# Two pool groups in steps beside the last two attention heads, squares through PSUM, key and query halves by transfer

## The chip, the cores and the metric

The kernel runs on one core of one Trainium2 chip. The metric is device microseconds of one execution. Before the change three runs took 2717.0 to 2720.67 us, median 2718.06 us.

The engines are named as in the profile: PE multiplies matrices (PEld is its weight load), DVE is the vector engine, ACT the activation engine, POOL the general engine, SP the engine that issues nearly all DMA transfers, in program order, as do all engines their own work.

## The reference, cut to what matters

One step of a network of two layers on 128 context tokens and 1024 latent tokens of width 1024, all in float32. Layer 0 is the mixer that the change touches:

```python
h = rmsnorm(x) * (1 + mod[1]) + mod[0]          # mod = silu(c) @ w_mod + b_mod, six parts of 1024
q, k, v, p = even_project(h, w_in, ...)         # 512 columns each; q and k get an rmsnorm per head (8 heads of 64)
a = neighbourhood_attention(q, k, v, cached keys and values, rpb)   # 8 rows x 16 columns, plus 256 cached keys
for g, w in enumerate((2, 4, 8, 16)):           # four pool groups of 128 channels
    d = window_mean(p[g], w) - p[g]
    y[g] = (d @ pool_w[g]) * pool_scale[g]
x = x + mod[2] * (concat(a, y) @ w_out)
x = x + mod[5] * conv_ffn(rmsnorm(x) * (1 + mod[4]) + mod[3])
```

Layer 1 has a convolution module in place of attention and pool, and the same feed-forward part.

## The kernel before, in words

Activations lie with features on the 128 partitions: eight tiles of 128 x 1154 (128 context tokens, 2 columns of gap, 1024 latent tokens). Each float32 product is three matmuls, of a high and a low part (`whi`, `wlo`, `hhi`, `hlo`): high x high, high x low, low x high. A weight unit of 128 x 1024 is loaded by SP, its high part is made by ACT, its low part by POOL (`wunit`, L246 to L258).

Layer 0 runs in `mixer0` in this order.

1. `start0` loads x, squares each of its eight tiles on ACT (L482) and sums the squares over features on PE (L484: nine matmuls with one column per tile, 72 in all). It also computes mod parts 0 and 1 in four quarters (`quarters`, L497 to L528; `modps` L502, `modt` L508), each of which gives two tiles of `hhi` and `hlo`.
2. `project_v` makes v in two passes over the eight tiles (L606 to L609). Beside it, and later, mod group (0, 1) is loaded and multiplied (`mod_group`, L292: sixteen loads of 512 KB, `mraw`, and 32 matmuls, `modps` L303).
3. The first query and key pair (`project_qk`), with the four pool groups in the order `PF = (1, 3, 2, 0)` between (`project_p`: 72 projection matmuls L454, window sums on DVE L554, high and low parts, then nine `pw` matmuls L584). Each pool group's last matmuls stand behind the next group's projection.
4. `attention`, 40 units: eight heads with one context unit and four latent units each. A unit has scores (`C`, `S`), a softmax, transposes (`tp` L852) and the weighted sum (`O`). In every unit `filler` is called twice. It advances the query and key projection of the next pair in heads 0 to 5, and mod group (0, 2) in heads 6 and 7 (`RM = 1` step per call). mod group (0, 2) uses six buffers, two each of the tags `wraw`, `whi` and `wlo`.
5. `split_half` prepares a head's operands: the keys in f32r once on the head's own 64 partitions (L678, ACT) and once on the other 64 (L680, DVE), the low part of the keys (POOL), the queries on the own partitions and their low part on the others (ACT, DVE), and a copy of the queries into `qm` (L691, POOL).
6. `trunk` reads back the eight tiles `cat` (four of attention, four of pool), splits them (L1286, L1287), and begins with the output projection: three output tiles together, the eight inputs in the order `[4, 5, 6, 7, 0, 1, 2, 3]`.

A scheduler with a model of times sets the final order on each engine. A transfer on SP that waits holds those behind it.

Of the kernel before, what the change touches and what calls it, by code (L numbers as in the profile page):

```python
# [39 lines left out]
PL = 8  # L40
PL0 = PL + NCTX + PL
PW = PL0 + NLAT + PL
WINS = (2, 4, 8, 16)
# [77 lines left out]
MS = 4  # L121
MT = 0
MI = 1.1
PF = (1, 3, 2, 0)
SEQ = (0, 0), (0, 1), (1, 0), (1, 1), (2, 0), (2, 1)
KP = 0
LP = 3
PP = 2
RM = 1
RQ = 3  # L130
EK = 0
ER = 1
# [26 lines left out]
class Beside:  # L159
# [24 lines left out]
    def finish(self):  # L184
        while self.parts:
            self.step()


class Kern:
# [43 lines left out]

    def wload(self, src):
        raw = self.wp.tile([P, 1024], F32, tag="wraw", name=self.nm("wraw"), bufs=2)
        self.nc.sync.dma_start(raw, src)
        for dst, lo in self.stores:
            self.nc.sync.dma_start(dst, lo)
        self.stores = []
        return raw  # L240

    def wunit(self, src, raw=None, eng=None, keep=None, kept=None):


        nc = self.nc
        if raw is None:  # L246
            raw = self.wload(src)
        hi = self.wp.tile([P, 1024], F32R, tag="whi", name=self.nm("whi"), bufs=self.wbufs)
        lo = self.wp.tile([P, 1024], F32R, tag="wlo", name=self.nm("wlo"), bufs=self.wbufs)
        if kept is not None:  # L250
# [206 lines left out]
    def start0(self, up, hp, ap, evac):  # L457


        nc = self.nc  # L460
        mm = nc.tensor.matmul
        xs, raws, wv = [], [], []
        nc.sync.dma_start(self.consts, self.i["consts"])
        for k in range(KT):
            x = up.tile([P, TS], F32, tag="u", name=f"x0_{k}")
# [5 lines left out]
        for i in range(16):  # L471
            raw = hp.tile([P, T], F32, tag="h", name=self.nm("mraw"))
# [2 lines left out]
            if i in (3, 7):  # L475
                wv.append(self.wload(self.i["wv"][i // 4]))
        st = [tok0(j) for j in range(9)]
        ms = self.psa.tile([P, 512], F32, tag="aux", name=self.nm("ms"))
        for k in range(KT):
            sq = ap.tile([P, 2, 640], F32, tag="prob", name=self.nm("sq"), bufs=2)  # L480
            sq = sq.rearrange("p a b -> p (a b)")[:, :T]
            nc.scalar.activation(sq, xs[k], AF.Square)  # L482
            for j, o in enumerate(st):
                mm(ms[:, j:j + 1], sq[:, o:o + P], self.cst("on"), start=k + j == 0, stop=k == KT - 1 and j == 8)  # L484
        r = self.rsqrt(ms[:, :9], 9)
        rb = self.psm.tile([P, 3, 512], F32, tag="mm3", name=self.nm("rb"))
        for j in range(9):
# [49 lines left out]
    def project_p(self, g, hhi, hlo, up):  # L537

        nc = self.nc
        w = WINS[g]  # L540
        ps = self.proj(self.wunit(self.i["wab"][g]), hhi, hlo)
        p = up.tile([P, TS], F32, tag="u", name=self.nm("p"))
        for o, n in ((0, PL), (PL + NCTX, PL), (PL0 + NLAT, PL)):
            nc.gpsimd.memset(p[:, o:o + n], 0.0)
        for pv, sv in self.psegs(ps, p, PL, PL0):
            nc.scalar.activation(sv, pv, AF.Copy)
        s, lo, hi = p, 0, PW
        step = 0
        while 2 ** (step + 1) <= w:
            a = 1 if step == 0 else 2 ** (step - 1)  # L550
            b = 0 if step == 0 else a
            nlo, nhi = lo + a, hi - b
            s2 = up.tile([P, TS], F32, tag="u", name=self.nm("ps"))
            nc.vector.tensor_tensor(s2[:, nlo:nhi], s[:, nlo - a:nhi - a], s[:, nlo + b:nhi + b], op=ALU.add)  # L554
            s, lo, hi = s2, nlo, nhi
            step += 1
        d = up.tile([P, TS], F32, tag="u", name=self.nm("pd"))
        nc.gpsimd.memset(d[:, NCTX:L0], 0.0)
        for (o, n, dst) in ((PL, NCTX, 0), (PL0, NLAT, L0)):
            nc.vector.scalar_tensor_tensor(d[:, dst:dst + n], s[:, o:o + n], 1.0 / w, p[:, o:o + n],  # L560
                                           op0=ALU.mult, op1=ALU.subtract)
        e0 = sum(x - 1 for x in WINS[:g])
        hw = w // 2
        edge = self.cst("edge")
        for (o, n, dst) in ((PL, NCTX, 0), (PL0, NLAT, L0)):
            for (c, m, eo) in ((0, hw, e0), (n - hw + 1, hw - 1, e0 + hw)):
                if m == 0:
                    continue
                tmp = self.cp.tile([P, 8], F32, tag="pedge", name=self.nm("pedge"), bufs=2)
                nc.vector.tensor_tensor(tmp[:, :m], s[:, o + c:o + c + m], edge[:, eo:eo + m], op=ALU.mult)  # L570
                nc.vector.tensor_tensor(d[:, dst + c:dst + c + m], tmp[:, :m], p[:, o + c:o + c + m],
                                        op=ALU.subtract)
        dh = up.tile([P, TS], F32R, tag="u", name=self.nm("pdh"))
# [4 lines left out]
        def finish():  # L578
            ps = self.psm.tile([P, 3, 512], F32, tag="mm3", name=self.nm("pw"))
            sl = slice(g * P, (g + 1) * P)  # L580
            for w_, x, a, b in ((self.pwhi, dh, True, False), (self.pwhi, dl, False, False),
                                (self.pwlo, dh, False, True)):
                for c, (o, n) in enumerate(CH):
                    nc.tensor.matmul(ps[:, c, :n], w_[:, sl], x[:, o:o + n], start=a, stop=b)  # L584
            y = up.tile([P, TS], F32, tag="u", name=self.nm("py"))
            for pv, sv in self.row3(ps, y):
                nc.scalar.activation(sv, pv, AF.Identity, scale=self.par("psc", g))
            nc.sync.dma_start(self.cat[4 + g], y[:, :T])
        return finish

    def project_v(self, hhi, hlo, ready, wv, sp, between):

# [71 lines left out]
    def split_half(self, q, k, b, new, res):  # L664


        nc = self.nc

        def lat(t):
            return t.rearrange("p (r g c) -> p r g c", g=4, c=16)  # L670

        def blk(t):
            return t.rearrange("p (g r c) -> p r g c", g=4, c=16)

        own = slice(64 * b, 64 * b + 64)
        oth = slice(64 - 64 * b, 128 - 64 * b)
        ks = new("ks")
        nc.scalar.activation(ks[own, :], k[own, :T], AF.Copy)  # L678
        yield
        nc.vector.tensor_copy(ks[oth, :], k[own, :T])  # L680
        nc.gpsimd.tensor_tensor(self.km[b][own, :], k[own, :T], ks[own, :].bitcast(F32), op=ALU.subtract)
        yield
        qs = new("qs")
        nc.scalar.activation(qs[own, :NCTX], q[own, :NCTX], AF.Copy)
        nc.scalar.activation(blk(qs[own, L0:T]), lat(q[own, L0:T]), AF.Copy)
        yield
        nc.vector.tensor_tensor(qs[oth, :NCTX], q[own, :NCTX], qs[own, :NCTX].bitcast(F32), op=ALU.subtract)
        nc.vector.tensor_tensor(blk(qs[oth, L0:T]), lat(q[own, L0:T]), blk(qs[own, L0:T]).bitcast(F32),
                                op=ALU.subtract)
        for o, e in ((0, NCTX), (L0, T)):  # L690
            nc.gpsimd.tensor_copy(self.qm[b][own, o:e], qs[own, o:e])  # L691
        res[b] = (qs, ks)
        yield

# [461 lines left out]
    def mixer0(self, dp):  # L1156
        tc, nc, I, cp = self.tc, self.nc, self.i, self.cp
        with ExitStack() as l0:
# [83 lines left out]
    def trunk(self):  # L1242
# [11 lines left out]
        with ExitStack() as st:  # L1254
# [242 lines left out]
```

## Time and profile before

| | us |
|---|---|
| median of three runs | 2718.06 |
| profiled execution, its time | 2718.41 |
| profiled execution, its span | 2716.6 |
| PE busy in the span | 2635.2 (97%) |
| DVE busy | 1605.9 (59%) |
| ACT busy | 1122.9 (41%) |
| POOL busy | 1260.9 (46%) |

The span runs from the first to the last instruction, and 1.8 us of the profiled execution lie around it. The mixer of layer 0 ends at 537.5 us, where the first matmul of the output projection begins. A "record" is one entry of PE in the trace; a float32 matmul of PE that isn't f32r has two. The granted clock (PEclk) is a share of 2.4 GHz, and 0.5 is the lower level of 1.2 GHz.

### The profile page before, as it was taken

The numbers are of one execution on the slowest core, as the hardware profiler recorded it, in microseconds if no ns is written. First come the engines' busy times: TensorE is split into PE (matmuls) and PEld (weight loads), VectorE is DVE, ScalarE is ACT, GpSimd is POOL, SyncE is SP. The second block draws the span as 40 slices with busy tenths as digits, with TensorE's granted clock in tenths as the row PEclk, the third lists the DMA queues.
The fourth block names the chain that finished last, engine by engine and source line by source line (L and its number), as shares of the span: only waits on it lengthen the run. The fifth ranks groups of instructions, "written<-read, shape, count | busy, mean of one in ns | idle before, by whom it ended". The sixth has DMA issues, their size and how long they took to land.

```text
span 2716.6 us, 38806 instructions
## 1 busy us (share of the span) xinstructions
PE 2635.2 (97%) x15108; PEld 2379.8 (88%) x15108; DVE 1605.9 (59%) x2456; ACT 1122.9 (41%) x1743; POOL 1260.9 (46%) x752
## 2 busy tenths in 40 slices
PE   8999998889999999999999999999999999999999
PEld 6688887688999999988998789989999999888887
DVE  2236777575476757663997854369974334444444
ACT  3325766525422222245555363555324323433332
POOL 1323444146433232225555353699756544655553
PEclk9999998999999999999999999999999999999999
DMA  7622214364446555544434553232222222433232
GB/s 266 198 76 69 56 53 131 92 223 146 145 150 202 175 174 192 193 147 156 142 133 144 178 179 116 85 88 77 70 74 70 77 85 71 125 93 93 93 95 92
DMA packets 137815, 341.17 MB, mean 126 GB/s; under 512 B 45728, under 2 KB 50976, under 8 KB 137632
## 3 DMA queue, kind: packets, MB, share of 16 engines
q1 hardware_dynamic: 137632, 338.69, 38.8%
q8 instruction: 120, 1.97, 0.3%
q14 instruction: 63, 0.52, 0.1%
HBM read 291.97 MB, written 46.67 MB: 125 GB/s over the span
## 4 chain that ended last, share of the span: by engine, by line
PE 80%; DVE 12%; DMA 3%; ACT 3%; issue 1%; POOL 1%; SPq 0%; POOLq 0%; DVEq 0%; ACTq 0%
PE mm L264 14%; PE mm L266 14%; PE mm L268 14%; PE mn L264 7%; PE mn L266 7%; PE mn L268 7%; DVE modacc L324 2%; DVE dacc L992 2%; PE mm L454 2%; DVE x L437 2%; PE O L884 1%; PE ms L484 1%; PE tp L852 1%; PE qps L634 1%; PE qps L636 1%
## 5 line engine op out<-in xcount | busy, mean ns | idle before, releaser
L254 POOL TENSOR_TENSOR wlo<-wraw,whi 128x1024 fp32r<-128x1024 f32 x280 | 686.0, 2455 | 926.1 <-ACT whi L252 792.6
L252 ACT ACTIVATE whi<-wraw 128x1024 fp32r<-128x1024 f32 x348 | 364.7, 1057 | 770.4 <-PE mm L266 404.5
L264 PE MATMUL mm<-h,whi 128*128 128x332 f32 (+6 forms) x2208 | 559.0, 324 | 11.5 <-DVE x L437 11.5
L268 PE MATMUL mm<-h,wlo 128*128 128x332 f32 (+6 forms) x2208 | 560.5, 324 | 0.4 <-POOL wlo L254 0.3
L266 PE MATMUL mm<-h,whi 128*128 128x332 f32 (+6 forms) x2208 | 559.5, 324 | 0.0
L264 PEld LDWEIGHTS mm<-h,whi 128*128 128x128 f32 x2208 | 383.0, 189 | 25.9 <-issue 12.8
L268 PEld LDWEIGHTS mm<-h,wlo 128*128 128x128 f32 x2208 | 381.3, 189 | 12.4 <-POOL wlo L254 0.9
L266 PEld LDWEIGHTS mm<-h,whi 128*128 128x128 f32 x2208 | 380.0, 189 | 10.4
L992 DVE SCALAR_TENSOR_TENSOR dacc<-u,params,dacc 128x661 f32<-128x661 f32 (+1 forms) x344 | 285.4, 830 | 7.7
L437 DVE SCALAR_TENSOR_TENSOR x<-mm,mod,x 128x128 f32<-128x128 f32 (+7 forms) x408 | 210.4, 561 | 128.3 <-PE mm L268 126.4
L264 PE MATMUL mn<-h,whi 128*128 128x494 f32 (+1 forms) x672 | 262.6, 391 | 3.2 <-DVE x L437 3.2
L266 PE MATMUL mn<-h,whi 128*128 128x494 f32 (+1 forms) x672 | 262.2, 390 | 0.0
L268 PE MATMUL mn<-h,wlo 128*128 128x494 f32 (+1 forms) x672 | 260.6, 390 | 0.0
L1088 DVE SCALAR_TENSOR_TENSOR facc<-mm,params,facc 128x663 f32<-128x663 f32 (+3 forms) x92 | 82.1, 892 | 275.3 <-ACT facc L1087 275.2
L1088 DVE SCALAR_TENSOR_TENSOR facc<-mn,params,facc 128x493 f32<-128x493 f32 (+1 forms) x84 | 62.0, 738 | 219.2 <-ACT facc L1087 219.1
L264 PE MATMUL mm<-fh,whi 128*128 128x332 f32 (+2 forms) x720 | 172.0, 318 | 15.0 <-DVE x L437 13.1
L268 PE MATMUL mm<-fh,wlo 128*128 128x332 f32 (+2 forms) x720 | 170.2, 316 | 0.0
L266 PE MATMUL mm<-fl,whi 128*128 128x332 f32 (+2 forms) x720 | 170.0, 316 | 0.0
L974 POOL TENSOR_TENSOR acc<-acc,tap 128x508 f32<-128x508 f32 (+1 forms) x104 | 151.2, 1457 | 37.1 <-ACT tap L973 31.2
L324 DVE SCALAR_TENSOR_TENSOR modacc<-mraw,sc,modacc 128x512 f32<-128x512 f32 x168 | 158.4, 992 | 0.1
L1100 POOL TENSOR_TENSOR facc<-facc,facc 128x494 f32<-128x494 f32 (+2 forms) x66 | 91.2, 1381 | 144.9 <-DVE facc L1090 136.8
L437 DVE SCALAR_TENSOR_TENSOR x<-mn,mod,x 128x510 f32<-128x510 f32 (+1 forms) x168 | 120.5, 737 | 63.7 <-PE mn L268 62.9
(227 smaller groups left out, 4520.5 us busy)
## 6 DMA issues: line engine op xcount, KB each, us to landing
wraw<-in_fi_dram SPq DMA_DIRECT2D x176, 512.0 KB
wraw<-in_fo_dram SPq DMA_DIRECT2D x88, 512.0 KB
mraw<-in_wmod_dram SPq DMA_DIRECT2D x48, 512.0 KB
mraw<-in_wmod_dram SPq DMA_DIRECT2D x96, 256.0 KB
wraw<-in_pw_dram SPq DMA_DIRECT2D x48, 512.0 KB
lowi<-wlo SPq DMA_DIRECT2D x44, 512.0 KB
wlo<-lowi SPq DMA_DIRECT2D x44, 512.0 KB
lowo<-wlo SPq DMA_DIRECT2D x22, 512.0 KB
```

The lines of the kernel that those rows point to most:

```text
L252: nc.scalar.activation(hi, raw, AF.Copy)
L254: (eng or nc.gpsimd).tensor_tensor(lo, raw, hi.bitcast(F32), op=ALU.subtract)
L264: mm(pv, whi, xhi[:, a:b], start=start, stop=False)
L266: mm(pv, whi, xlo[:, a:b], start=False, stop=False)
L268: mm(pv, wlo, xhi[:, a:b], start=False, stop=stop)
L324: i = nc.vector.scalar_tensor_tensor(acc, rv, c, acc, op0=ALU.mult, op1=ALU.add)
L437: nc.vector.scalar_tensor_tensor(xd[:, a:b], pv, gate[:, d, st:st + 1], xd[:, a:b], op0=ALU.mult, op1=ALU.add)
L454: mm(ps[:, c, :n], w[:, s], x[k][:, o:o + n], start=a, stop=b)
L974: nc.gpsimd.tensor_tensor(acc[:, :n], acc[:, :n], p[:, :n], op=ALU.add)
L992: nc.vector.scalar_tensor_tensor(acc[:, :n] if t == NCK - 1 else pacc, u[:, t:t + n], wk(i, t), acc[:, :n] if t == side else pacc, op0=ALU ...
L1088: nc.vector.scalar_tensor_tensor(acc[:, 1:W], part.ps(ps, 0, W - 1), w(0), acc[:, 1:W], op0=ALU.mult, op1=ALU.add)
L1100: (nc.gpsimd if side or part.n == 1 else nc.vector).tensor_tensor(a[:, :W], a[:, :W], g[:, :W], op=ALU.mult)
```

## The change

The squares: the first tile is squared into SBUF, the other seven into two PSUM tiles, and DVE adds each to the first. PE then sums once, with nine matmuls.

Pool groups 3 and 2 (`PF = 3, 2`) stay ahead of the attention. Groups 0 and 1 (`PS = 0, 1`) become a generator, `project_p_steps`, that `filler` advances in heads 6 and 7, two steps per call (`RM = 2`), with mod group (0, 2) behind them in the list. Each loads its pool weights again. Their matmuls use the one PSUM buffer `psg`.

The keys on the other 64 partitions and the queries in `qm` are written by DMA from SP instead of by DVE and POOL. The attention's preparation takes four steps (`PP = 4`) behind each of the two pool groups that stay. The output projection takes its inputs in the order `[6, 7, 0, 1, 2, 4, 5, 3]`.

```diff
-PF = (1, 3, 2, 0)
+PF = 3, 2
+PS = 0, 1
-PP = 2
-RM = 1
+PP = 4
+RM = 2
@@ start0
-        ms = self.psa.tile([P, 512], F32, tag="aux", name=self.nm("ms"))
-        for k in range(KT):
-            sq = ap.tile([P, 2, 640], F32, tag="prob", name=self.nm("sq"), bufs=2)
+        acc = ap.tile([P, 2, 640], F32, tag="prob", name=self.nm("sq"), bufs=2)
+        acc = acc.rearrange("p a b -> p (a b)")[:, :T]
+        nc.scalar.activation(acc, xs[0], AF.Square)
+        for k in range(1, KT):
+            sq = self.psm.tile([P, 3, 512], F32, tag="mm3", name=self.nm("sq"))
             sq = sq.rearrange("p a b -> p (a b)")[:, :T]
             nc.scalar.activation(sq, xs[k], AF.Square)
-            for j, o in enumerate(st):
-                mm(ms[:, j:j + 1], sq[:, o:o + P], self.cst("on"), start=k + j == 0, stop=k == KT - 1 and j == 8)
+            nc.vector.tensor_tensor(acc, acc, sq, op=ALU.add)
+        ms = self.psa.tile([P, 512], F32, tag="aux", name=self.nm("ms"))
+        for j, o in enumerate(st):
+            mm(ms[:, j:j + 1], acc[:, o:o + P], self.cst("on"), start=True, stop=True)
...
+    def project_p_steps(self, g, hhi, hlo, up, psp, tag):
...
+        whi, wlo = self.wunit(self.i["wab"][g])
...
+        for c, (o, n) in enumerate(CH):
+            ps = psp.tile([P, 512], F32, tag=tag, name=self.nm("pps"))
+            for k in range(KT):
+                s = slice(k * P, (k + 1) * P)
+                mm(ps[:, :n], whi[:, s], hhi[k][:, o:o + n], start=k == 0, stop=False)
+                mm(ps[:, :n], whi[:, s], hlo[k][:, o:o + n], start=False, stop=False)
+                mm(ps[:, :n], wlo[:, s], hhi[k][:, o:o + n], start=False, stop=k == KT - 1)
+                if k == 3:
+                    yield
...
+        for d in self.pooled(g, p, up):
+            yield
+        dh, dl = self.halves(d, up)
+        pwhi, pwlo = self.wunit(self.i["pw"])
+        yield
...
+        for o, n in CH:
+            ps = psp.tile([P, 512], F32, tag=tag, name=self.nm("ppw"))
...
+            nc.scalar.activation(y[:, o:o + n], ps[:, :n], AF.Identity, scale=self.par("psc", g))
+        nc.sync.dma_start(self.cat[4 + g], y[:, :T])
+        yield
...
@@ split_half
-        nc.vector.tensor_copy(ks[oth, :], k[own, :T])
+        nc.sync.dma_start(ks[oth, :].bitcast(F32), ks[own, :].bitcast(F32))
...
-            nc.gpsimd.tensor_copy(self.qm[b][own, o:e], qs[own, o:e])
+            nc.sync.dma_start(self.qm[b][own, o:e].bitcast(F32), qs[own, o:e].bitcast(F32))
@@ mixer0
-                mods = [self.mod_group(0, 2, self.wp, self.psg, evac, tag="g", last=(self.pst, "w"))]
+                mods = [self.project_p_steps(g, hhi, hlo, up, self.psg, "g") for g in PS]
+                mods += [self.mod_group(0, 2, self.wp, self.psg, evac, tag="g", last=(self.pst, "w"))]
@@ trunk
-            order = [4, 5, 6, 7, 0, 1, 2, 3]
+            order = [6, 7, 0, 1, 2, 4, 5, 3]
```

`pooled` and `halves` hold the window sums and the split that stood in `project_p`, unchanged.

The first rows of PE, before (`ms` the sums of squares, `modps` the first quarter of mod, `mraw` its loaded weights):

```order
L484 MATMUL ms_233<-consts,sq_267 128x1 x9
L502 MATMUL modps_339<-mraw_197,sc 32x512 x2
L484 MATMUL ms_233<-consts,sq_278 128x1 x9
L484 MATMUL ms_233<-consts,sq_289 128x1 x9
L502 MATMUL modps_339<-mraw_199,sc 32x512 x2
L502 MATMUL modps_339<-mraw_201,sc 32x512 x2
L502 MATMUL modps_339<-mraw_203,sc 32x512
L484 MATMUL ms_233<-consts,sq_300 128x1 x9
```

And now (`rb` is the broadcast of the inverse roots):

```order
L491 MATMUL ms_256<-consts,sq_233 128x1 x9
L509 MATMUL modps_283<-mraw_197,sc 32x512 x2
L509 MATMUL modps_283<-mraw_199,sc 32x512 x2
L509 MATMUL modps_283<-mraw_201,sc 32x512 x2
L509 MATMUL modps_283<-mraw_203,sc 32x512 x2
L497 MATMUL rb_270<-consts,rsr_267 128x130
L497 MATMUL rb_270<-consts,rsr_267 128x128 x8
L515 MATMUL modt_294<-consts,modev_292 128x2 x4
```

Sixty-three matmuls are gone, and the first quarter of mod stands ahead of the broadcast.

PE in head 7, before: the matmuls of mod group (0, 2) (`modps_4548`) lie one load at a time among the units.

```order
L303 MATMUL modps_4548<-mraw_5045,sc 32x512 x2
L852 MATMUL tp_4733<-consts,prob_4625 128x128 x2
L303 MATMUL modps_4548<-mraw_5081,sc 32x512 x2
L697 MATMUL C_4774<-ck_4272,qs_4366 128x256
L698 MATMUL C_4774<-ck_4272,qm_155 128x256
L697 MATMUL C_4774<-ck_4272,qs_4366 128x256
L698 MATMUL C_4774<-ck_4272,qm_155 128x256
L303 MATMUL modps_4548<-mraw_5129,sc 32x512 x2
```

Now all 32 (`modps_4870`) stand in one piece behind the last matmuls of pool group 1 (`ppw_4864`), and the transposes and sums of the last two units behind them. This is where the piece begins:

```order
L602 MATMUL ppw_4864<-pdh_4834,whi_4840 128x384
L603 MATMUL ppw_4864<-pdl_4835,whi_4840 128x384
L604 MATMUL ppw_4864<-pdh_4834,wlo_4841 128x384
L306 MATMUL modps_4870<-mraw_4871,sc 32x512 x2
L306 MATMUL modps_4870<-mraw_4919,sc 32x512 x2
L306 MATMUL modps_4870<-mraw_4923,sc 32x512 x2
L306 MATMUL modps_4870<-mraw_4959,sc 32x512 x2
```

Twelve rows on it ends with the last load, and the attention goes on:

```order
L306 MATMUL modps_4870<-mraw_5205,sc 32x512 x2
L346 MATMUL modt_5211<-consts,modev_5209 128x8 x4
L912 MATMUL tp_5218<-consts,prob_5100 128x128 x4
L912 MATMUL tp_5227<-consts,prob_5100 128x128 x4
L912 MATMUL tp_5236<-consts,prob_5100 128x128 x2
```

SP at the same place, before (`cat_66` a store of the attention's third pair, `vr` values of a unit, `woab` the output projection's weights): the loads of mod group (0, 2) end ahead of head 7's values.

```order
L300 DMA mraw_5045<-in_wmod_dram 128x1024
L300 DMA mraw_5081<-in_wmod_dram 128x1024
L300 DMA mraw_5129<-in_wmod_dram 128x1024
L898 DMA cat_66<-ao_3778 128x1154
L785 DMA vr_4850<-vd 128x1x64 x4
L785 DMA vr_4995<-vd 128x1x64 x4
L1284 DMA cat_5423<-cat_66 128x664
L236 DMA wraw_5491<-in_woab_dram 128x1024
```

And now (`cat_69` is pool group 1's result, stored from `py_4853` and read back into `cat_5391`):

```order
L303 DMA mraw_4981<-in_wmod_dram 128x1024
L606 DMA cat_69<-py_4853 128x1154
L303 DMA mraw_4985<-in_wmod_dram 128x1024
L303 DMA mraw_5021<-in_wmod_dram 128x1024
L303 DMA mraw_5025<-in_wmod_dram 128x1024
L303 DMA mraw_5073<-in_wmod_dram 128x1024
L1345 DMA cat_5391<-cat_69 128x664
L303 DMA mraw_5077<-in_wmod_dram 128x1024
L303 DMA mraw_5113<-in_wmod_dram 128x1024
```

Four more mod loads follow, and then the `woab` loads. Ahead of `mraw_4981` stand `mraw_4871`, `mraw_4919`, `mraw_4923`, `mraw_4963`, six reads of `cat` and `mraw_4959`. From the output projection on, all engines have the order that they had.

## Rows read from the trace of the kernel before

**Rows 1.** Page, busy time of PE, and the costliest groups (busy, mean ns).

```profile
PE 2635.2 (97%) x15108; PEld 2379.8 (88%) x15108; DVE 1605.9 (59%) x2456; ACT 1122.9 (41%) x1743; POOL 1260.9 (46%) x752
...
L437 DVE SCALAR_TENSOR_TENSOR x<-mn,mod,x 128x510 f32<-128x510 f32 (+1 forms) x168 | 120.5, 737 | 63.7 <-PE mn L268 62.9
```

**Rows 2.** Windows by stage: length, busy by engine (records), granted clock, DMA share, GB/s.

```profile
0.00:56.60 56.60, 48.98 (x228) 37.92 (x228) 8.93 (x20) 18.16 (x22) 5.36 (x12) 1.00 0.85 314
56.60:93.60 37.00, 36.94 (x178) 28.96 (x182) 28.37 (x39) 15.16 (x22) 11.76 (x6) 1.00 0.17 50
93.60:223.00 129.40, 125.92 (x713) 104.73 (x713) 35.14 (x56) 38.20 (x58) 37.35 (x32) 1.00 0.46 145
223.00:235.50 12.50, 9.15 (x42) 8.01 (x40) 8.88 (x12) 6.24 (x12) 5.40 (x5) 0.83 0.24 90
235.50:449.50 214.00, 204.94 (x1439) 188.71 (x1440) 160.56 (x419) 141.15 (x391) 79.16 (x61) 0.98 0.23 61
449.50:465.50 16.00, 10.26 (x69) 6.42 (x68) 15.71 (x17) 11.87 (x25) 15.43 (x11) 0.82 0.71 190
465.50:537.50 72.00, 61.97 (x359) 45.06 (x359) 45.64 (x136) 41.92 (x121) 16.19 (x13) 0.87 0.32 103
```

**Rows 3.** Groups by line, PE, 0 to 56.6 us (busy, mean ns, idle before).

```profile
L484 PE MATMUL ms<-consts,sq 128*128 128x1 f32 x144 | 31.2, 352 | 6.4 <-ACT sq L482 6.4
```

**Rows 4.** Timeline, 0 to 70 us: start, length, engine (ACT, POOL, PE).

```profile
7.94 1.17 ACT L482 ACTIVATE sq<-x 128x1154 f32<-128x1154 f32 x1 [1.57 <-DMA x<-in_x_dram]
...
23.94 1.06 ACT L252 ACTIVATE whi<-wraw 128x1024 fp32r<-128x1024 f32 x1 [0.76 <-DMA wraw<-in_wv_dram]
...
43.23 1.81 POOL L371 TENSOR_TENSOR rsr<-rsv,mhalf 128x9 f32<-128x9 f32 x1 [41.83 <-DVE rsv L368]
...
47.29 3.37 PE L502 MATMUL modps<-mraw,sc 128*32 128x512 f32 x16
50.60 2.27 PE L490 MATMUL rb<-consts,rsr 128*128 128x130 f32 x18
```

**Rows 5.** DMA view, 0 to 130 us: rate in 40 slices of 3.25 us.

```profile
GB/s 106 351 408 419 412 412 407 415 405 417 406 387 97 109 310 345 66 0 0 81 0 0 106 61 35 129 0 72 90 263 394 284 283 197 199 279 291 309 419 364
```

**Rows 6.** Chain that ended last, in order of time: start, length, what.

```profile
209.74 12.27 PE mm L454 x69
...
297.30 2.25 DMA vr<-vd
...
364.35 3.62 DMA mraw<-in_wmod_dram
...
539.03 3.96 DMA cat<-ao
```

**Rows 7.** Timeline, later places: DVE and PE at 209 to 230 us, then 455 on.

```profile
209.60 2.53 DVE L554 TENSOR_TENSOR ps<-p 128x1175 f32<-128x1175 f32 x1 [4.59 <-ACT p L546]
212.16 2.79 DVE L554 TENSOR_TENSOR ps<-ps 128x1173 f32<-128x1173 f32 x2
...
230.29 0.79 PE L584 MATMUL pw<-pdh,pwhi 128*128 128x386 f32 x3 [2.29 <-ACT pdh L575]
...
455.47 3.95 DVE L680 CAST ks<-qk 64x1154 fp32r<-64x1154 f32 x2
...
457.90 18.21 SPq L300 DMA_DIRECT2D mraw<-in_wmod_dram  x10
...
529.06 1.93 PE L852 MATMUL tp<-consts,prob 128*128 128x128 f32 x8
```

**Rows 8.** Line L680: count, min/median/max ns, first and last start.

```profile
L680 DVE CAST ks<-qk x8: 758/2008/3146, 219.9 to 456.3; 64x1154 fp32r<-64x1154 f32 x8
```

**Rows 9.** Groups by line, PE, 465.5 to 537.5 us.

```profile
L303 PE MATMUL modps<-mraw,sc 128*32 128x512 f32 x40 | 11.2, 696 | 0.0
```

**Rows 10.** Waits of PE in 465.5 to 537.5 us: total, times, longest.

```profile
PE O L879 <- DVE ptl L857: 7.0, 5, 2.8
```

**Rows 11.** Waits of SP, 430 to 545 us: total, times, longest.

```profile
SPq L898 <- DVE ao L895: 32.2, 2, 27.0
```

More of the change, by code (lines that the diff above doesn't have):

```diff
@@ L235, in wload @@
         raw = self.wp.tile([P, 1024], F32, tag="wraw", name=self.nm("wraw"), bufs=2)
+        raw = raw[:, :src.shape[1]]
         self.nc.sync.dma_start(raw, src)
@@ L249, in wunit @@
         lo = self.wp.tile([P, 1024], F32R, tag="wlo", name=self.nm("wlo"), bufs=self.wbufs)
+        hi, lo = hi[:, :src.shape[1]], lo[:, :src.shape[1]]
         if kept is not None:
@@ L539, in project_p @@
         nc = self.nc
-        w = WINS[g]
         ps = self.proj(self.wunit(self.i["wab"][g]), hhi, hlo)
@@ L546, in project_p, with finish @@
             nc.scalar.activation(sv, pv, AF.Copy)
+        for d in self.pooled(g, p, up):
+            pass
+        dh, dl = self.halves(d, up)
+        def finish():
+            ps = self.psm.tile([P, 3, 512], F32, tag="mm3", name=self.nm("pw"))
+            sl = slice(g * P, (g + 1) * P)
+            for w_, x, a, b in ((self.pwhi, dh, True, False), (self.pwhi, dl, False, False),
+                                (self.pwlo, dh, False, True)):
+                for c, (o, n) in enumerate(CH):
+                    nc.tensor.matmul(ps[:, c, :n], w_[:, sl], x[:, o:o + n], start=a, stop=b)
+            y = up.tile([P, TS], F32, tag="u", name=self.nm("py"))
+            for pv, sv in self.row3(ps, y):
+                nc.scalar.activation(sv, pv, AF.Identity, scale=self.par("psc", g))
+            nc.sync.dma_start(self.cat[4 + g], y[:, :T])
@@ new lines, in project_p @@
+        return finish
+    def project_p_steps(self, g, hhi, hlo, up, psp, tag):
+        nc = self.nc
+        mm = nc.tensor.matmul
+        whi, wlo = self.wunit(self.i["wab"][g])
+        p = up.tile([P, TS], F32, tag="u", name=self.nm("p"))
+        for o, n in ((0, PL), (PL + NCTX, PL), (PL0 + NLAT, PL)):
+            nc.gpsimd.memset(p[:, o:o + n], 0.0)
+        for c, (o, n) in enumerate(CH):
+            ps = psp.tile([P, 512], F32, tag=tag, name=self.nm("pps"))
[6 more added lines that the diff above has]
+                    yield
+            if c == 0:
+                nc.scalar.activation(p[:, PL:PL + NCTX], ps[:, :NCTX], AF.Copy)
+                nc.scalar.activation(p[:, PL0:PL0 + 256], ps[:, L0:386], AF.Copy)
+            else:
+                nc.scalar.activation(p[:, PL0 + o - L0:PL0 + o - L0 + n], ps[:, :n], AF.Copy)
+            yield
+        for d in self.pooled(g, p, up):
+            yield
+        dh, dl = self.halves(d, up)
+        pwhi, pwlo = self.wunit(self.i["pw"])
+        yield
+        y = up.tile([P, TS], F32, tag="u", name=self.nm("py"))
+        sl = slice(g * P, (g + 1) * P)
+        for o, n in CH:
+            ps = psp.tile([P, 512], F32, tag=tag, name=self.nm("ppw"))
+            mm(ps[:, :n], pwhi[:, sl], dh[:, o:o + n], start=True, stop=False)
+            mm(ps[:, :n], pwhi[:, sl], dl[:, o:o + n], start=False, stop=False)
+            mm(ps[:, :n], pwlo[:, sl], dh[:, o:o + n], start=False, stop=True)
+            nc.scalar.activation(y[:, o:o + n], ps[:, :n], AF.Identity, scale=self.par("psc", g))
+        nc.sync.dma_start(self.cat[4 + g], y[:, :T])
+        yield
@@ L547, in project_p, with pooled @@
+    def pooled(self, g, p, up):
+        nc = self.nc
+        w = WINS[g]
         s, lo, hi = p, 0, PW
@@ L556, in project_p @@
             step += 1
+            yield None
         d = up.tile([P, TS], F32, tag="u", name=self.nm("pd"))
@@ L572, in project_p, with halves @@
                                         op=ALU.subtract)
+        yield d
+    def halves(self, d, up):
+        nc = self.nc
         dh = up.tile([P, TS], F32R, tag="u", name=self.nm("pdh"))
@@ L576, in project_p @@
         nc.vector.tensor_tensor(dl[:, :T], d[:, :T], dh[:, :T].bitcast(F32), op=ALU.subtract)
[L578 to L589, printed above, removed]
+        return dh, dl
     def project_v(self, hhi, hlo, ready, wv, sp, between):
```

## The prediction

> **What bounds the kernel now.** I read three views in turn: busy time, the stretches of layer 0's mixer, and inside a stretch the timeline and the chain of waits. PE is busy 97% of the span [rows 1], so a change helps where it takes work from PE or fills PE's idle time. The table of stretches shows where that idle time lies [rows 2]: 7.6 us before 56.6 (the start; there the first pass of v sets in), almost none in the first pass of v, 3.5 us to 223, 3.4 us at the seam of dense stage and attention (223 to 235.5), 9.1 us in heads 0 to 5, 5.7 us at 449.5 to 465.5, where DVE is busy 15.7 of 16 us, and 10.0 of the 72 us of heads 6 and 7. In the last two the granted clock is 0.82 and 0.87, so some of the busy time is slow time as well. From 537.5 on every engine keeps its order, so the forecast is the shift of that point, 537.5, where the output projection begins. All sums are of the profiled execution (2718.41 us), which lies 0.35 us above the median.
>
> **The squares.** Before, PE sums the squares in 144 records, 31.2 us, 0.217 us each [rows 3]. Of 72 matmuls 9 stay, 18 records, 3.9 us, and 27.3 us of PE work go. But PE can begin only when DVE has added all eight tiles. The second square starts at 7.94, when its tile lands; the next tiles follow at 0.59 MB each by the rate of some 410 GB/s [rows 4, 5], 1.44 us apart, so the eighth lands near 16.6 and is squared by 17.8. The seven additions with one operand in PSUM don't stand in the trace. By the nearest row, 737 ns for 510 columns from PSUM [rows 1], one of 1154 columns takes about 1.6 us; one after another from 9.1 they end near 20.3. PE's first work thus moves from 6.4 to 20.3.
>
> Then PE has the sums (to 24.2) and the first quarter's mod matmuls, whose weights land before that, since the load behind them is there at 23.9 [rows 4]. These take 3.4 us at the rate of 47.29 [rows 4]; I allow up to twice that. The inverse root (1.8) hides there. The broadcast takes 2.3 us [rows 4], again at most twice that. From its end to v passed 3.7 us before (50.60 + 2.27 to 56.6), and the same steps stand there now. So v begins near 37, not 56.6. But two quarters of mod now lie inside the pass, not one: 3.4 + 0.9 us more. End of the pass: 19.6 - 4.3 = 15 us earlier. The other account, 27.3 us of work less 13.9 us of later begin, gives 13.4. I take -14, with bounds -18 (fast rate, additions hidden) and -8 (additions at 2.5 us each, as a group's first window sum takes, [rows 7], in part behind arriving tiles).
>
> **The dense stage.** One group's projection is 72 matmuls, 69 of them in 12.27 us [rows 6], 0.178 each: 12.8 us, and nine more for the pool weights, 1.6. Two groups leave a stretch in which PE is busy 126 of 129 us: -28.8. At the seam the last group was the one of window 2; now it is window 8, with two window sums more on DVE, 2.79 us together [rows 7], in a chain on which PE already waits 2.3 us. I take +3 (0, if the next projection's matmuls cover it, to +6).
>
> **Keys and queries by transfer.** Eight copies of keys leave DVE, 0.76 to 3.1 us each, median 2.0 [rows 8], and POOL loses the copies of queries. The worst place is 455.47: two in a row, 3.95 us, while the softmax and PE wait [rows 7]. Against this stand 24 transfers more. Their size, 0.3 MB from SBUF to SBUF, isn't in the trace; the nearest rows are 2.25 us for a small read and 3.96 for 0.59 MB [rows 6], so 3 us each, several units ahead of their use. I take -5 of the 14.8 us of idle time in the two stretches to 465.5, with bounds -10 and +6 (where SP, held by a query that isn't ready, brings the values of a unit late).
>
> The Trainium skill speaks against this part (page "DMA: Bandwidth & Descriptors", section "Anatomy of one DMA"): a transfer's wait for a semaphore is spent in the issuing sequencer, ahead of the dispatch. The trace agrees: SP stood 27.0 us at one store of attention output [rows 11], and nothing behind it was issued. By that rule each new transfer can hold the queue, and the +6 above would be the sum's value; by the row alone, which came at a place with nothing urgent behind it, the cost is nothing.
>
> **Heads 6 and 7 up to the end of pool group 1 (call it E).** Before, 72 us: 62.0 busy, of it 11.2 of mod group (0, 2) [rows 2, 9], so 50.8 of attention. The transposes and sums of the last two units, 8.5 us (529.06 to 537.5, [rows 7]), come after E now. That leaves 42.3, at a clock of 0.87; with PE better filled I take 40.5. The pool groups bring 28.8, of which a first third (4.3) goes into the hole at 449.5, where mod matmuls stood: 24.5 remain. Idle time: PE waited 7.0 us for DVE's low parts in these heads [rows 10], and the fillers cover that except in the units with few of them, 3 us; and group 1's last chain (two window sums of 2.5 and 1.4 us [rows 7], the difference, the edges and the two splits: some 10 us by estimate, among softmax work) have 7 us of attention beside them, and cost 6. E is 40.5 + 24.5 + 9 = 74 us after head 6's begin.
>
> **After E.** Here the change adds a wait. Mod group (0, 2) is now one piece of 32 matmuls on PE behind E. It has six buffers, and two of its first six loads need buffers that group 1's pool weights hold until E, so 12 of 16 loads start after E. Among them on SP stand the store of group 1's result, which waits for ACT, and its read back, which waits for the store (4.0 us by [rows 6]). Bytes: 12 x 0.52 + 0.59 + 0.34 = 7.2 MB, at 410 GB/s 17.6 us, and some 2 to 3 us until the last one is seen (one load alone takes 3.6, [rows 6]): 20 us. By the other row, ten such loads in 18.21 us [rows 7], it is 22. PE has some 7 us of work in that time and waits the rest. Queued behind it on PE are the spread of mod (1.5 us) and the last two units (8.5), behind them on ACT and POOL the first output weights, which arrive just in time. So the output projection starts 30 us after E; bounds 24 and 42.
>
> **Sum.** Heads 6 and 7: 74 + 30 = 104 in place of 72, +32. With the rest: -14 - 28.8 + 3 - 5 + 32 = -12.8. 2718.4 - 12.8 = 2705.6 in the profiled execution; for the median **2706 us**.
>
> **Rivals.**
> 1. *The mod piece decides: slower.* Place: PE between E and the last two units. If SP stands at the read back of group 1's result and the last six loads go out only then, one at a time as buffers come free (1.8 us each by [rows 7], after 4 us of store and 4 of read), and group 1's window sums come 5 us later than I assume because DVE has pool and softmax at once, heads 6 and 7 take 74 + 5 + 42 = 121, +49, and the sum is +4; with half of the start's gain gone, +11. Time 2722 to 2729, say 2724. It decides from about 45 us of added time in heads 6 and 7. For it: the order of SP, which puts the six loads behind the read back. Against it: PE's buffers free one after another anyway, and the rate of 410 GB/s has been seen over 30 us. Chance 0.18.
> 2. *The piece is nearly hidden, and DVE's relief counts more.* If E comes late against the loads or the fillers remove all of the idle time in heads 6 and 7 (-9) and the clock there returns to 1.0 (-4), and keys give -8, the sum is -12.8 - 9 - 4 - 3 = -29: 2690. For it: 14.8 + 10 us of idle time and a clock of 0.87. Against it: twelve loads can't start before E. Chance 0.24.
> 3. *The squares give nothing.* If the additions take 2.5 us each, PE's begin moves to 27, and quarters 2 and 3 then hold PE inside the pass: the start gives -2 and the sum is near -1: 2717, no change that can be measured. Against it: nothing in that stretch but two weight splits stands on DVE. Chance 0.08.
>
> **How the numbers follow.** My own case has 0.50; its own range is 2699 to 2713. No change means within 0.2% (5.4 us), about what a measurement of this kernel can tell. Faster: 0.48 of my case and rival 2's 0.24: 0.72. Slower: nearly all of rival 1, 0.15. The remaining 0.13 is no change: rival 3 and the edges of the others. The range for 8 in 10 goes from rival 2's value to the near end of rival 1: 2688 to 2722.
>
> **What would show it.** In the profile after: PE's first matmul near 20 us and the first v matmul near 37; the dense stage's end some 43 us earlier (near 180 us, not 223); no `ks` work on DVE; in heads 6 and 7 projection matmuls of the pool groups in every second unit and a clock near 1.0; then a stretch of about 20 us in which PE has only mod matmuls and waits for `mraw`; the output projection's first matmul near 525. I am wrong if PE doesn't stand for `mraw` there, if the v pass begins after 45, or if the output projection begins after 535.

## The result

The changed kernel takes 2725.64 us (median of 15 runs, 2721.48 to 2729.44), the kernel before 2718.21 (median of 15, 2712.59 to 2722.09): ratio 1.0027, 95% interval 1.002 to 1.0035. The change makes the kernel 0.27% slower; 2706 was forecast. The profiled execution took 2724.37 us, span 2722.6, 6.0 more than that of before.

Busy time of the engines on the page of the changed kernel, against [rows 1]:

```profile
PE 2611.9 (96%) x14982; PEld 2351.0 (86%) x14982; DVE 1614.7 (59%) x2455; ACT 1125.6 (41%) x1749; POOL 1248.3 (46%) x738
```

PE is busy for 23.3 us less and is yet later: its idle time is 110.7 us (2722.6 - 2611.9) in place of 81.4. Where it lies, the windows by stage say. They are cut at v's first matmul, q's first matmul, the first score, head 6's first score, the end of pool group 1's ppw (E), the end of the mod piece and the output projection's first matmul; columns as in [rows 2]. Before, v, q, the first score, head 6 and the output projection begin at 55.4, 116.1, 233.8, 465.5 and 537.5; the cuts of [rows 2] are others in part.

```profile
0.00:31.00 31.00, 12.51 (x77) 8.05 (x77) 13.70 (x19) 15.06 (x16) 3.23 (x9) 1.00 0.96 375
31.00:105.90 74.90, 70.36 (x309) 46.64 (x306) 34.30 (x47) 24.94 (x36) 21.79 (x14) 0.95 0.62 200
105.90:197.90 92.00, 81.35 (x484) 69.18 (x482) 28.84 (x42) 28.75 (x47) 25.59 (x20) 0.98 0.40 121
197.90:423.30 225.40, 214.74 (x1497) 196.97 (x1497) 164.38 (x429) 147.78 (x406) 72.19 (x57) 0.97 0.26 61
423.30:512.80 89.50, 70.00 (x410) 61.12 (x410) 60.05 (x146) 51.17 (x138) 23.98 (x22) 0.88 0.26 78
512.80:535.60 22.80, 18.35 (x64) 2.70 (x64) 0.00 (x0) 0.76 (x2) 1.59 (x1) 0.74 0.98 358
535.60:544.40 8.80, 7.59 (x60) 6.71 (x61) 6.51 (x12) 6.20 (x10) 4.74 (x2) 1.00 0.38 115
```

Head 6 begins at 423.3, 42.2 us earlier than the 465.5 of before; heads 6 and 7 then take 121.1 us (89.5 + 22.8 + 8.8) in place of 72. The output projection starts at 544.4, not 537.5, and the rest of the program takes what it took (2178.2 us, 2179.1 before). So all of the loss is in the last two heads.

The start, in the timeline of PE (start, length, line, operation), answers to [rows 4]:

```profile
18.50 4.00 PE L491 MATMUL ms<-consts,sq 128*128 128x1 f32 x18 [18.50 <-DVE sq L488]
22.42 3.64 PE L509 MATMUL modps<-mraw,sc 128*32 128x512 f32 x16
25.99 2.41 PE L497 MATMUL rb<-consts,rsr 128*128 128x130 f32 x18
...
30.97 0.50 PE L666 MATMUL vps<-whi,hhi 128*128 128x512 f32 x1
```

The additions end at 18.4 and v begins at 31, not 55.4: 24.5 us earlier, more than the 19.6 forecast.

The last two heads, in the timeline of DVE and PE from 489 us, against [rows 6, 7]:

```profile
489.69 1.38 DVE L620 TENSOR_TENSOR ps<-p 128x1175 f32<-128x1175 f32 x1 [0.93 <-ACT p L591]
...
497.82 1.62 DVE L637 TENSOR_TENSOR pedge<-ps,consts 128x2 f32<-128x2 f32 x2
...
535.62 0.69 DVE L343 COPY modev<-modps 128x512 f32<-128x512 f32 x1 [28.50 <-PE modps L306]
```

```profile
505.38 0.69 PE L602 MATMUL ppw<-pdh,whi 128*128 128x386 f32 x1 [8.79 <-ACT pdh L647]
...
512.85 5.21 PE L306 MATMUL modps<-mraw,sc 128*32 128x512 f32 x20 [0.67 <-ACT py L605]
519.54 1.05 PE L306 MATMUL modps<-mraw,sc 128*32 128x512 f32 x4 [1.47 <-DMA mraw<-in_wmod_dram]
...
529.40 1.05 PE L306 MATMUL modps<-mraw,sc 128*32 128x512 f32 x4 [0.23 <-DMA mraw<-in_wmod_dram]
```

Two holes stand there. Group 1's window sums begin at 489.7, its first ppw matmul at 505.4, 15.7 us later, and PE waits 8.79 us for it, since the last two units' transposes stand behind ppw and the mod piece on its queue (the softmax of the first of them was done at 488.8). Then the piece itself: DVE has nothing for 28.5 us. SP's own rows show when its loads go out: the last two of the first four at 488.9, behind them the reads of `cat` (to 501.2), and twelve only from 511.9 on, the end of the ppw matmuls, whose weights hold the buffers.

```profile
488.92 0.80 SPq L303 DMA_DIRECT2D mraw<-in_wmod_dram  x2
489.78 11.46 SPq L1345 DMA_DIRECT2D cat<-cat  x6
511.89 0.81 SPq L303 DMA_DIRECT2D mraw<-in_wmod_dram  x2
512.83 0.35 SPq L606 DMA_DIRECT2D cat<-py  x1
514.82 3.48 SPq L303 DMA_DIRECT2D mraw<-in_wmod_dram  x4
521.54 0.33 SPq L1345 DMA_DIRECT2D cat<-cat  x1
521.92 6.38 SPq L303 DMA_DIRECT2D mraw<-in_wmod_dram  x6
```

### The profile page after: what moved, and what is told of

The parts are those of the page before. It is cut to its first block, busy times and chain, and to the rows that moved or that the text cites. A ratio compares the mean times of both kernels' runs of the same rounds, so it can differ in the third digit from the quotient of the medians.

```text
span 2722.6 us, 38622 instructions
## 1 busy us (share of the span) xinstructions
PE 2611.9 (96%) x14982; PEld 2351.0 (86%) x14982; DVE 1614.7 (59%) x2455; ACT 1125.6 (41%) x1749; POOL 1248.3 (46%) x738
## 4 chain that ended last, share of the span: by engine, by line
PE 80%; DVE 11%; DMA 3%; ACT 2%; issue 1%; POOL 1%; SPq 0%; POOLq 0%; DVEq 0%; ACTq 0%
PE mm L267 15%; PE mm L271 14%; PE mm L269 14%; PE mn L267 8%; PE mn L269 8%; PE mn L271 7%; DVE modacc L327 2%; DVE x L440 2%; PE O L944 1%; DVE dacc L1052 1%; PE qps L694 1%; PE qps L695 1%; PE qps L696 1%; DMA mraw<-in_wmod_dram 1%; PE tp L912 1%
## 5 line engine op out<-in xcount | busy, mean ns | idle before, releaser
L267 PE MATMUL mm<-h,whi 128*128 128x332 f32 (+6 forms) x2208 | 558.7, 324 | 11.2 <-DVE x L440 11.2
L267 PEld LDWEIGHTS mm<-h,whi 128*128 128x128 f32 x2208 | 383.2, 189 | 25.7 <-issue 12.5
L269 PEld LDWEIGHTS mm<-h,whi 128*128 128x128 f32 x2208 | 379.8, 189 | 10.4
```

The source lines that it names most:

```text
L267: mm(pv, whi, xhi[:, a:b], start=start, stop=False)
L269: mm(pv, whi, xlo[:, a:b], start=False, stop=False)
```

## Experiments

Each kernel was timed in five rounds beside the kernel before. Stages are told by four events of the profiled execution: q's first matmul, the first score, the third store of attention output (the end of head 5, some 16 us after head 6's first score) and the output projection's first matmul. One caution: kernels with the same start had q's first matmul between 102.6 and 107.7 us, so a few us in one stage of one execution mean nothing. And the scheduler orders each kernel anew: stages that an edit doesn't touch can change with it.

| kernel | median us | ratio to before (95%) | to q | to first score | to third store | to output proj. |
|---|---|---|---|---|---|---|
| before | 2718.2 | | 116.1 | 117.7 | 247.5 | 56.2 |
| squares alone | 2703.7 | 0.9955 (0.994 to 0.9969) | 106.6 | 122.5 | 244.1 | 50.5 |
| transfers alone | 2706.2 | 0.9967 (0.9955 to 0.998) | 114.0 | 116.3 | 237.8 | 51.9 |
| pool steps alone | 2738.1 | 1.0079 (1.0066 to 1.0091) | 113.7 | 90.5 | 243.5 | 107.5 |
| squares and transfers | 2700.9 | 0.9944 (0.9931 to 0.9956) | 102.6 | 119.6 | 239.5 | 54.1 |
| squares and pool steps | 2743.5 | 1.0095 (1.0081 to 1.0109) | 105.7 | 91.9 | 250.2 | 113.6 |
| transfers and pool steps | 2734.9 | 1.0065 (1.0052 to 1.0079) | 113.7 | 92.3 | 240.3 | 103.5 |
| changed kernel | 2725.6 | 1.0027 (1.002 to 1.0035) | 105.9 | 92.0 | 242.6 | 104.0 |

### The parts alone

```
-acc, additions through PSUM            (squares as before: 72 ms matmuls)
+nc.vector.tensor_copy(ks[oth, :], ..); nc.gpsimd.tensor_copy(self.qm[b][own, o:e], ..)   (copies as before)
+PF = (1, 3, 2, 0); PS = (); PP = 2; RM = 1; order = [4, 5, 6, 7, 0, 1, 2, 3]             (pool groups as before)
```

Each of the first three kernels keeps one part and undoes the other two by these edits.

> The kernel before with one part of the change: the squares summed through PSUM, so that 9 ms matmuls stand where 72 stood. Theory A (the start is lost again to what follows: in the changed kernel v's first matmul came 24.5 us earlier, q's first matmul 10.3 us): q's first matmul about 10 us earlier than the 116.11 of before and a time 8 to 12 us below the kernel before. Rival B (the squares' gain stays whole, and all of the loss is in heads 6 and 7): 20 to 24 us below. Rival C (the squares give nothing in the end, my third rival): within 3 us of before.

> The kernel before with one part of the change: the copies for keys (DVE) and queries (POOL) as DMA transfers on SP's queue. By the prediction's step 5 us below before. Rival: each transfer is a wait of some 2 us ahead of the half's scores (in the changed kernel PE waited 1.17 us for ks and 0.49 us for qm at 423 to 425 us), and the copies lay beside other work anyway: 0 to 6 us above before.

> The changed kernel with the squares and the copies as before, so that the pool groups in steps stand alone. Theory A (the stage of heads 6 and 7 costs more than the dense stage gives): third cat store to output projection about 105 us against 58, dense stage 26 to 29 us shorter, in all 12 to 20 us above before. Rival B (pool steps are about neutral and the transfers lose): within 4 us of before.

Squares alone: -14.1 us, a little over theory A and far from B. By the profile 9.6 of it lie ahead of q; 5.7 lie behind the third store, where the edit changes nothing but the scheduler made another order. Transfers alone: -11.6, more than twice the step's 5; the rival falls. The pool steps alone: +20.3. Theory A holds, just over its range: dense stage -27, from third store to output projection 107.5 us against 56.2. So two parts of three gain and the third loses more than both.

### Parts in pairs

> The changed kernel with all four pool groups in the dense stage as before, so squares and transfers together. Theory A (the pool groups in steps are what made the change slower; the other two parts gain 14 and 12 us alone and touch different stages): the two gains add, 22 to 28 us below before, about 2692. Rival B (they share a gain, since either one runs into the next wait): 12 to 18 us below before, no better than the better one alone.

> The changed kernel with the copies for keys and queries back on DVE and POOL (squares and pool steps stay). From the parts alone (-14 and +20) 2724. Theory A: with pool steps the seam into attention has DVE and POOL as its chain (in the pool steps alone, first score to first cat store took 102.6 us against 87.7 of before, in the changed kernel 86.6), so the copies cost more here: 2728 to 2738, slower than the changed kernel. Rival B: the transfers wait on SP's queue behind the mod loads and the copies do as well: 2718 to 2725, the same as the changed kernel or below.

> The changed kernel with the squares as before (72 ms matmuls). From the parts alone (-12 and +20) 2727. Theory A (the squares' gain stays in every order): 10 to 15 us above the changed kernel, 2736 to 2740. Rival B (the gain is lost in the changed kernel to the later stages, since the parts alone add up to 5 us below before and the whole is 7 above): within 4 us of the changed kernel.

Squares and transfers take 2700.86 us: faster than both kernels, by 25 us than the changed one. The gains overlap (-16, not -26), as rival B says; why they do isn't shown. Squares and pool steps without transfers take 2743.5 us, above the range of theory A; transfers and pool steps without squares 2734.88, 9 us above the changed kernel, just short of A's 10. In every pairing the pool steps lose: +20 alone, +40 with the squares, +29 with the transfers, +25 with both. Beside pool steps with copies the squares give nothing (2743.5 against 2738.1): their 8.0 us up to q are lost again, 6.7 in heads 0 to 5 and 6.1 behind them. Why isn't settled.

### How many groups, and the mod group

```
-PF = 3, 2;  PS = 0, 1
+PF = 3, 2, 1;  PS = (0,);  PP = 3;  order = [5, 6, 7, 0, 1, 2, 4, 3]          (one group in steps)
-mods += [self.mod_group(0, 2, ...)]
+mods.insert(1, self.mod_group(0, 2, ...))                     (mod between the groups; a second one with RM = 3)
-for m in range(3)
+for l, m in ((0, 2), (1, 0), (1, 1), (1, 2))                  (mod group made in the trunk on DVE; MS = 6)
```

> The changed kernel with one pool group (0) in steps beside heads 6 and 7 and three (3, 2, 1) in the dense stage. Theory A (a group takes the same 14 us of TensorE wherever it stands, the dense stage had no idle TensorE and heads 6 and 7 only some 10 us of it, so the first group costs little and the second costs all of its time and more): from the third cat store to the output projection about 75 us against 56 of before and 104 of the changed kernel, in all 2695 to 2706, 20 to 30 us below the changed kernel. Rival B (both groups cost alike, half of 48 us each against 14 in the dense stage): 2706 to 2712. Rival E (the mod piece behind the pool steps is what costs, whatever the number of groups): the piece stays and the time is above 2712.

One group: 2711.97 us, 0.9981 (0.9972 to 0.999), so 11 above none and 14 below two; rival B's range, at its edge. The stage shows more than the time: 72.8 us, as A says, after 54.1 with no group and 104.0 with two. The first adds 18.7, the second 31.2. The mod matmuls don't stand in one piece here but in eight among head 7's units, so rival E, which has the piece stay, falls.

> The changed kernel without the mod group (0,2) in heads 6 and 7: its sum is made in the trunk beside the output projection's first part, on DVE (as those of layer 1 are), with 6 steps a tile instead of 4. Theory A (what the piece behind the pool steps costs is its own 22.8 us, since nothing else runs beside it): the output projection begins 18 to 24 us earlier than in the changed kernel (544.4), the trunk gives back 0 to 10 of it to DVE, the time is 2702 to 2712. Rival B (the last two units, whose transposes stand behind the piece, and the pool chain keep the end where it is): output projection at 535 or later, time within 6 us of the changed kernel.

> Squares and transfers with all pool groups in the dense stage, and mod group (0,2) made in the trunk on DVE. Theory A (TensorE bounds heads 6 and 7, 17 us of mod matmuls leave it): output projection 8 to 15 us earlier than the 515.6 of squares and transfers alone, time 2688 to 2697. Rival B (heads 6 and 7 are then bound by the softmax chain, and DVE in the output projection is late for the norm behind it): 2699 to 2708.

> As the one before, with pool group 0 in steps beside heads 6 and 7 where the mod matmuls were. Theory A (a group fills TensorE's idle time there once the mod group is gone): 10 us from the dense stage, no more than 8 us more in heads 6 and 7: 2 to 8 us below the same with all groups in the dense stage. Rival B (a group costs some 11 us net beside the heads, as it did with the mod group there): 5 to 15 us above it.

All three moved the mod sum into the trunk and were slow for that: 2743.83, 2743.07 and 2736.05 us (1.0093, 1.0087, 1.0065). From the output projection's first matmul to the end they take 2225 to 2231 us in place of 2178. My expectation of 0 to 10 us lost in the trunk was wrong. The groups of DVE, with two groups in steps, from 512 to 660 us (count, busy, mean ns); in the changed kernel the same stretch behind its output projection has 40 and 8 of them:

```profile
L327 DVE SCALAR_TENSOR_TENSOR modacc<-mraw,sc,modacc 128x512 f32<-128x512 f32 x56 | 57.8, 1090 | 6.3 <-DMA mraw<-in_wmod_dram 6.1
L325 DVE TENSOR_SCALAR modacc<-mraw,sc 128x512 f32<-128x512 f32 x12 | 14.7, 1290 | 0.0
```

and of PE's waits there (total, times, longest), that it was waited for; in the changed kernel only the second of these three stands in that stretch, with 11.2 us:

```profile
PE ms L383 <- DVE sq L409: 9.8, 1, 9.8
PE mm L267 <- DVE x L440: 8.2, 3, 3.8
PE modps L333 <- DVE modacc L327: 4.3, 1, 4.3
```

These waits are a part of the 53 us that this kernel loses behind the output projection; 30 are lost in the first 170 us and nearly all of the rest some 650 to 735 us behind it. With two groups the output projection began 32 us earlier than in the changed kernel, more than A's 24. With none it began at 516.6, not earlier than the 515.6 of squares and transfers: the stage was 10.0 us shorter, but the stages ahead of it took 11 more in this execution.

For the stage of heads 6 and 7 they are good measurements all the same. From third store to output projection, no group, all pool work in the dense stage, then two groups, the mod group in the trunk both times:

```profile
472.50:516.60 44.10, 37.67 (x265) 31.23 (x263) 33.87 (x105) 33.27 (x100) 5.85 (x7) 1.00 0.12 36
```

```profile
437.70:512.30 74.60, 59.98 (x368) 52.27 (x366) 52.36 (x133) 47.99 (x124) 19.13 (x19) 0.93 0.20 66
```

| third store to output projection, us | no group | one | two |
|---|---|---|---|
| mod group in the trunk | 44.1 | 54.2 | 74.6 |
| mod group beside the heads | 54.1 | 72.8 | 104.0 |

Attention alone needs 44.1 us from the third store on, with 6.4 us of idle PE. One thing beside it, mod group or pool group, adds 10 us (a little over the 8 of theory A in the last of the three; its time, 7 us below the one with no group, is inside A's range). Two things add 29 to 31 us, three 60. A pool group costs 10.1 us there without the mod group and 18.7 with it. So what room there was beside heads 6 and 7 was taken already: by the mod group.

> The changed kernel with mod group (0,2) between pool group 0 and pool group 1 in the list that the filler draws from, where it was behind both. On PE its matmuls then stand in small pieces among head 6's units, and the last ppw matmuls stand behind the last unit's O. Theory A (the 22.8 us piece in which PE has only mod matmuls and DVE stands still for 28.5 us is what made the change slower): the piece goes, 12 to 20 us faster than the changed kernel (about 2705 to 2713). Rival D (pool group 1's own chain from pps to ppw, 16 us at 489 to 505, then ends the stage behind the last unit): within 5 us of the changed kernel.

> The changed kernel with the mod group between the pool groups and three steps a draw instead of two, so that group 1's steps end three units earlier and its ppw matmuls stand among the last two units' O. Theory A (with the group between and two steps a draw, group 1's chain from pps to ppw stood alone behind the last unit, where PE was busy for 5.9 of 17 us): 6 to 12 us of it go, third cat store to output projection 80 to 86 us against 92.2, the time about 2706. Rival B (the stage is bound by the sum of its work and the order changes little): within 4 us of the 2715.7 of two steps a draw.

2715.68 us (0.9995, 0.9985 to 1.0005) with the mod group between: 10 us below the changed kernel, less than A said, with 92.2 us for the stage. The 22.8 us piece is gone, and group 1's chain stands behind the last unit in its place (rival D), as PE's row and the window show:

```profile
527.98 0.69 PE L602 MATMUL ppw<-pdh,whi 128*128 128x386 f32 x1 [2.41 <-ACT pdh L647]
```

```profile
520.00:537.00 17.00, 5.90 (x15) 3.78 (x15) 8.90 (x16) 6.21 (x10) 7.97 (x5) 0.55 0.65 197
```

With three steps a draw that hole is gone, but PE waits for `mraw` in head 7 (2.4 and 3.0 us at the longest), the stage takes 94.7 us and the whole 2719.69 (1.0009, 0.9999 to 1.0018). Rival B: neither of these two orders wins it back.

### The piece's loads, and POOL beside group 1's edges

```
-nc.sync.dma_start(raw, self.i["wmod"][l, m, k, :, ...])       (for m == 2)
+raw = self.raw0 after the first load
```

> The changed kernel in which mod group (0,2) loads one of its 16 pieces and uses it for all 16 (it leaves out 15 loads of 512 KB; matmuls and their place stay). Theory A (the piece behind the pool steps waits for its loads, which stand behind it on SP's queue): the 22.8 us of the piece fall to the 17 us of its 64 matmul records at 0.26 us, the time by 5 to 8 us, the rest of the 29 us that the group costs behind two pool groups being its matmuls with nothing beside them. Rival B (the loads cost nothing, PE's clock after the idle time does): within 2 us of the changed kernel.

2712.87 us, 0.9986 (0.9977 to 0.9995): 12.8 below the changed kernel, and the output projection at 531.9 in place of 544.4. PE's row of the piece:

```profile
513.76 9.08 PE L312 MATMUL modps<-mraw,sc 128*32 128x512 f32 x64 [0.67 <-ACT py L611]
```

64 records in 9.08 us, not the 17 of my expectation. The 0.26 us a record that I had read as their price is what the four records of one load take when they stand alone (1.05 us; the kernel before has such fours without a wait for loads too). Here the records of two loads start together, four every 0.42 us at a granted clock of 1.00.

The rival, the clock, can be read off the piece of the changed kernel. It ran at 0.50 and then at 1.00:

```profile
522.10:528.10 6.00, 5.77 (x16) 0.75 (x16) 0.00 (x0) 0.76 (x1) 0.45 (x1) 0.50 1.03 413
528.10:535.60 7.50, 6.32 (x24) 0.86 (x24) 0.00 (x0) 0.00 (x0) 1.14 (x1) 1.00 1.01 404
```

At either clock PE took up a load each 1.28 us (from 522.2 to 526.0, and from 528.1 on), and the DMA engines moved about the same, 413 and 404 GB/s: this is the pace of the loads. So the loads behind E cost some 13 us: theory A, but more than its 5 to 8.

```
-nc.gpsimd.tensor_tensor(lo, c, hi, op=ALU.subtract)
+(nc.vector if part is OA else nc.gpsimd).tensor_tensor(lo, c, hi, op=ALU.subtract)
```

> The changed kernel with the low halves of the trunk's cat tiles of the first part (L1348) on DVE instead of POOL. In the changed kernel five of them ran on POOL at 497.2 to 505.5 us, just while DVE made the edges of pool group 1 (L637, L638: pairs of 1.6, 1.0, 1.1 and 1.6 us where group 0's took 0.21 a pair), and PE stood idle for 8.79 us ahead of the last ppw. Theory A (POOL beside DVE slows these small operations): the edge pairs fall to 0.2 to 0.5 us, the idle time ahead of ppw by 3 to 5 us, the time by 2 to 5 us. Rival B (the eight DVE operations take the same time from the chain that they give back): within 2 us of the changed kernel.

The edges ran fast, and PE waited about as long as before:

```profile
499.30 0.23 DVE L637 TENSOR_TENSOR pedge<-ps,consts 128x2 f32<-128x2 f32 x2
499.44 0.84 DVE L1348 TENSOR_TENSOR h<-cat,h 128x664 fp32r<-128x664 f32 x1
```

```profile
506.60 0.69 PE L602 MATMUL ppw<-pdh,whi 128*128 128x386 f32 x1 [8.53 <-ACT pdh L647]
```

2726.85 us (1.0031, 1.0019 to 1.0043). From the first window sum to the first ppw matmul it is 15.4 us after 15.7. Rival B: what POOL's work cost the edges, DVE pays for the subtractions, 0.84 us each, which stand between them.

## Why the prediction was wrong

**The step that failed is heads 6 and 7 up to E.** It put E 74 us after head 6's begin, as 40.5 of attention, 24.5 of pool matmuls and 9 idle. It is 89.5: 19.5 idle, 31.0 of pool matmuls and, by difference, 39.0 of attention. So attention was right, and the idle time and the pool matmuls were not. Cut at group 1's first window sum and at its first ppw matmul the stretch reads:

```profile
423.30:489.70 66.40, 60.35 (x367) 54.45 (x367) 42.80 (x118) 39.30 (x114) 12.15 (x14) 0.95 0.21 58
489.70:505.40 15.70, 5.31 (x38) 4.27 (x36) 15.58 (x27) 9.55 (x21) 9.19 (x7) 0.74 0.59 197
505.40:512.80 7.40, 4.34 (x9) 2.41 (x9) 1.67 (x3) 2.31 (x4) 2.65 (x2) 0.50 0.00 0
```

Of the waits of PE in heads 6 and 7 these are the longest (total, times, longest), against [rows 10]:

```profile
PE ppw L602 <- ACT pdh L647: 8.8, 1, 8.8
PE modps L306 <- DMA mraw<-in_wmod_dram: 4.4, 8, 1.6
PE O L939 <- DVE ptl L917: 4.0, 3, 2.1
```

Group 1's last chain was taken as some 10 us, with 7 of attention beside it and yet 6 idle (10 less 7 would have left 3), and its nine ppw matmuls as 1.6 us. The chain is 15.7, the last units stand behind it on PE's queue, and 10.4 of it are idle. The nine matmuls take 7.4: they go through the one buffer `psg` in three parts, PE is idle for 3.1 us of that, waiting for ACT and DVE, and the granted clock is 0.50. That is 13.5 us idle in place of 6; ahead of the chain it is 6.0 in place of 3. I had counted on a clock near 1.0; it was 0.88 in the whole stretch, 0.95 ahead of the chain. No run takes the bare chain away (8.5 and 9.6 us of it are bare in the two runs of the last experiments), so what it costs is read from the trace alone.

That the two groups don't pay by themselves the forecast had: -25.8 in the dense stage and the seam against +32 in heads 6 and 7. Measured it is -25.7 against +49.1. The dense stage kept PE busy 126 of 129 us, so a group moved from there gains its matmuls and no more, and heads 6 and 7 had 10.0 us idle [rows 2] with the mod group in place, for two groups of 14.4 each. By these rows the move could win 10 us at the most, an estimate, and each wait that it adds comes off that.

**After E** was right: 31.6 us against 30, with twelve loads behind E and PE waiting for `mraw`. The cost was known and booked; some 13 of it are the loads. Since E came late, the output projection began at 544.4, where the forecast had 525 and called itself wrong from 535 on.

**The squares**: -14 forecast, -14.1 alone, and that they agree is luck. Up to q, where the forecast had it, the gain is 9.6 us alone and 10.3 in the changed kernel; alone the rest comes from stages behind it that were ordered anew. The terms were off in both directions. v begins 24.5 us earlier, not 19.6 (the forecast's 56.6 is v's third matmul, the first stands at 55.4), but from there to q it takes 74.9 us in place of 60.7, 14 more where 4.3 were booked: the mod matmuls take 16.8 us there in place of 9.2, PE waits 3.2 us there for DVE's low half, and the clock is 0.95.

**The transfers**: -5 forecast, -11.6 alone, just outside the bounds of -10 and +6. The rule of the Trainium skill that I weighed against this part (page "DMA: Bandwidth & Descriptors", section "Anatomy of one DMA": the wait is spent in the issuing sequencer) didn't decide: of waits for `ks` and `qm` PE shows 1.2 and 0.5 us in the changed kernel, both at head 6's begin, and 2.2 and 0.8 with the transfers alone. So the sum goes by the row, not by the +6.

**Dense stage and seam**: -25.8 forecast; q's first matmul to first score went from 117.7 to 92.0, -25.7.

Up to head 6 the sum was thus -44.8 forecast and -42.2 measured: 10.3 up to q, 25.7 to the first score and 6.3 in heads 0 to 5. Rival 1 had the total of heads 6 and 7 (121) and the time (2722 to 2729), but by other terms: 42 us after E, where 31.6 were needed, and an E only 5 us later, where it came 15.5 later. That its total fits is luck.

## What to carry to other kernels

Before moving work from a stage in which an engine is full to one in which it has gaps, look at what already fills the gaps, and count only what is left: more than that can't be won, and every wait that the move adds comes off it. The last item in such a row of fillers is to be priced apart, since what stands behind it on the engine's queue waits with it, for its chain and for its loads. And the parts of a change are worth timing alone: two of these three gained 16 us together.

## What was not expected of the hardware

What 64 mod records cost hangs on when their loads arrive: 18.35 us busy in 22.8 load by load, and 9.08 when the operand lies there, at nearly the same granted clock (0.74 and 0.77). And small operations of DVE can suffer beside POOL: a pair of 128x2 edges took 1.62 us while POOL subtracted five 128x664 tiles, and 0.23 when that work stood on DVE itself; operations of 64x256 on DVE took 0.40 to 0.42 us either way.
